# A two-layer hybrid trunk on one core: chunk scan by transition matrices, attention kept by token, substitution in PSUM, another step order, FFN sums copied from PSUM

## The chip, the cores and the metric

The kernel runs on one core of a Trainium2 chip. The metric is the device time of one execution in microseconds (us): the median of three runs of the kernel before was 2342.84 us (2339.17 to 2346.02). A profile was taken of one more execution.

## The reference, cut to what matters

Two layers work on a residual h of 512 tokens by 1024. In each, a feed-forward half-step (FFN a), a mixer, a second feed-forward half-step (FFN b) and a gated embedding (PLE) follow each other; the first three end in a layer norm. The mixer has three groups of heads on one projection: gated DeltaNet (8 heads of 64), stick-breaking attention (4 heads) and latent attention (4 heads). The change touches two of them:

```python
# DeltaNet, chunks of 64 tokens; lhs is unit lower triangular
u = triangular_solve(lhs, vc * beta)
w = triangular_solve(lhs, kb * exp(gc))
def step(state, xs):
    v_new = u_n - w_n @ state
    o_n = qd_n @ state + qk_n @ v_new
    state = state * gl_n + kd_n.T @ v_new
    return state, o_n
# latent attention, 4 blocks of 128 queries
s = (qn @ kn.T + qr @ kr.T) * scale, masked causally
o = softmax(s) @ v
```

## The kernel before, in words

All work is in `trunk`. TensorE (PE) multiplies; the precise products of weights are three fp32r matmuls (a high part, a low part and a cross part, L398 to L400 and L404 to L406), and the small products inside the heads are plain fp32, where one 64x64 matmul is two records in the trace. A framework puts the instructions into an order on each engine and sets the semaphores. Within the mixer the order that it starts from is the string `order` in `OPT`, one per layer, whose words are steps (`inv1` is `eliminate`, `uw2` is `u_w(2)`, `la13` is `latent(1, 3)`, `sc0` is `scan(0)`); the table `eng` says which engine copies or scales. PSUM is four pools of two banks: `psI` (`ibank()`, for the projections), `psA` (`bank()`), `psB` (`banks()`) and `psC` (`banks(True)`).

The steps that the change and the prediction touch, by their lines:

- **Inverse of lhs.** `inverse` (L911) turns the 16-row blocks onto partitions. `eliminate` (L926) does 15 steps of forward substitution on DVE, each a product (L936) and a sum (L937), on tiles `pr`, `X` and `inv_t` in SBUF. `turned` turns them back (L943, L944), and `inverse32` and `inverse64` double the block size with tiny matmuls (L955, L961). Beside it PE does the projection of the latents (`in_latent`), the values (`in_values`) and `keys`, whose transposes (L999) need the queries scaled by `decayed_queries` (`dq`, L893 on DVE).
- **u and w.** `u_w(t)` (L1000) makes u (L1007) and, with 64x64 products (L1016), w already transposed into `KQ`; a POOL multiplication (L643) scales by token in between.
- **Scan.** `scan(t)` goes through two chunks of 64 tokens. Per chunk: 16 matmuls with the old state (L1083), two DVE subtractions giving `vn`, 8 matmuls for the new state (L1096), a DVE sum, 8 matmuls on `vn` for the output (L1103), two ACT copies.
- **Latent attention.** `latent(h2, qt)` does two heads for 128 queries: scores (L801, L802), a maximum, its product with -scale (L805), exp on ACT with the sum, a division of the whole row of weights (L809), transposes (L811), a copy, and the product with the values (L818), whose result stands by channel.
- **Gates and out.** `gate_out` multiplies the normed scan output with the gate on POOL (L1133) and transposes it (L1166); `split_heads` makes high and low parts for the out-projection (L1139, L1140).
- **FFN front.** `build_xT(t)` transposes h (L258), and `split_from_psum` gives its high part by an ACT cast (L250) and its low part by DVE (L251). The FFN then sums the two parts again into `xf`, four pieces of 128x1024, two on POOL and two on DVE (L455), for the Strassen-like sums t1 to t4.

## Time and profile before

| what | value |
|---|---|
| median of three runs | 2342.84 us (2339.17 to 2346.02) |
| the profiled execution | 2345.6 us, its span 2343.9 us |
| mean granted TensorE clock | 0.976 of full speed |
| PE busy | 2265.5 us, 97% |
| DVE, ACT, POOL busy | 1379.9, 1043.0, 895.9 us (59, 44, 38%) |
| chain that ended last | PE 89%, DVE 7%, issue 2% |
| mixer of layer 0, of layer 1 | about 381 to 758 us, 1560 to 1920 us of the span |

PE is the engine to look at, but its 97% is a mean: in the FFNs it does not stop, and its idle time and its lower clock stand in the mixers and at the fronts of FFNs. A busy share of PE says nothing about the speed, so the granted clock belongs to each window. Where a line of a helper (L79, L250) stands in a row, the tile names tell which step called it.

### The profile page before, as it was taken

What the parts mean: (1) busy time and instruction counts of PE and PEld (TensorE: products, weight loads), DVE (VectorE), ACT (ScalarE), POOL (GpSimd) and SP (SyncE); (2) the same over time, 40 slices, a digit from 0 to 9 for tenths busy, and PEclk for the clock granted to TensorE, in tenths of its full rate; (3) what the DMA queues carried; (4) which work ended last, traced back from release to release, by engine and by line L of the source; (5) the groups of instructions that cost most, each with busy time, mean ns of one, the idle gap of its engine ahead of it and who ended that gap; (6) DMA issues with size and microseconds to landing.
All of it is one profiled execution on the core that took longest, in us unless ns stands there. A gap on an engine that the chain in (4) does not pass through costs nothing.

```text
span 2343.9 us, 40415 instructions
## 1 busy us (share of the span) xinstructions
PE 2265.5 (97%) x16834; PEld 1999.3 (85%) x16834; DVE 1379.9 (59%) x2027; ACT 1043.0 (44%) x1743; POOL 895.9 (38%) x491
## 2 busy tenths in 40 slices
PE   7999999998988999999999999999989889999999
PEld 7999888766877899988789998887678679999887
DVE  8877316657465877632667773166573758776333
ACT  4555423653442455532335554237534434556222
POOL 5222552433344522245442225524333554223442
PEclk9999999999989999999999999999989889999999
DMA  5332342212013133233413323422120121333331
GB/s 162 100 109 90 117 126 57 67 37 69 20 38 99 46 117 101 83 122 118 126 33 108 102 95 107 127 64 58 37 69 20 46 90 56 115 100 104 113 99 63
DMA packets 186792, 199.88 MB, mean 85 GB/s; under 512 B 10128, under 2 KB 151536, under 8 KB 186608
## 3 DMA queue, kind: packets, MB, share of 16 engines
q1 hardware_dynamic: 186608, 197.29, 27.7%
q8 instruction: 132, 2.16, 0.4%
q14 instruction: 52, 0.43, 0.1%
HBM read 195.17 MB, written 2.10 MB: 84 GB/s over the span
## 4 chain that ended last, share of the span: by engine, by line
PE 89%; DVE 7%; issue 2%; DMA 1%; POOL 1%; ACT 1%; SPq 0%; POOLq 0%; DVEq 0%; ACTq 0%
PE pi L398 6%; PE pi L400 6%; PE pi L399 6%; PE pc L406 4%; PE pc L405 4%; PE pc L404 4%; PE pa L406 3%; PE pa L405 3%; PE pa L404 3%; PE pb L405 3%; PE pb L406 3%; PE pb L404 3%; PE pc L398 2%; PE pc L399 2%; PE pc L400 2%; PE pi L406 2%
## 5 line engine op out<-in xcount | busy, mean ns | idle before, releaser
L79 POOL TENSOR_TENSOR wlo<-wraw,whi 128x1024 fp32r<-128x1024 f32 (+4 forms) x169 | 355.7, 2115 | 404.0 <-ACT whi L77 397.0
L77 ACT CAST whi<-wraw 128x1024 fp32r<-128x1024 f32 (+2 forms) x162 | 167.0, 1034 | 347.1 <-PE pa L400 176.7
L99 POOL TENSOR_TENSOR wlo<-wq,whi 128x1024 fp32r<-128x1024 f32 x48 | 126.2, 2629 | 288.2 <-ACT whi L98 275.8
L98 ACT CAST whi<-wq 128x1024 fp32r<-128x1024 f32 x116 | 121.7, 1049 | 132.2 <-issue 34.5
L99 POOL TENSOR_TENSOR wlo<-wraw,whi 128x1024 fp32r<-128x1024 f32 x32 | 86.1, 2691 | 226.3 <-ACT whi L98 178.1
L404 PE MATMUL pb<-x,whi 128*128 128x256 f32 x448 | 128.9, 290 | 2.1 <-ACT x L250 2.1
L405 PE MATMUL pb<-x,whi 128*128 128x256 f32 x448 | 130.0, 291 | 0.0
L406 PE MATMUL pb<-x,wlo 128*128 128x256 f32 x448 | 128.7, 288 | 0.0
L98 ACT CAST whi<-wraw 128x1024 fp32r<-128x1024 f32 x84 | 88.1, 1049 | 90.5 <-issue 25.5
L99 DVE TENSOR_TENSOR wlo<-wq,whi 128x1024 fp32r<-128x1024 f32 x68 | 87.1, 1281 | 68.0 <-ACT whi L98 68.0
L405 PE MATMUL pc<-x,whi 128*128 128x256 f32 x448 | 126.8, 284 | 0.0
L404 PE MATMUL pc<-x,whi 128*128 128x256 f32 x448 | 126.8, 284 | 0.0
L406 PE MATMUL pc<-x,wlo 128*128 128x256 f32 x448 | 126.5, 283 | 0.0
L98 ACT CAST whi<-s 128x1024 fp32r<-128x1024 f32 x80 | 83.8, 1048 | 62.5 <-PE pc L405 33.6
L99 DVE TENSOR_TENSOR wlo<-s,whi 128x1024 fp32r<-128x1024 f32 x80 | 110.8, 1385 | 1.3 <-ACT whi L98 1.2
L295 DVE SCALAR_TENSOR_TENSOR h<-h,pi 128x512 f32<-128x512 f32 x12 | 8.2, 684 | 167.3 <-PE pi L400 167.3
L398 PE MATMUL pi<-x,whi 128*128 128x512 f32 x256 | 103.8, 405 | 0.0
L400 PE MATMUL pi<-x,wlo 128*128 128x512 f32 x256 | 103.5, 404 | 0.0
L399 PE MATMUL pi<-x,whi 128*128 128x512 f32 x256 | 103.3, 403 | 0.0
L99 DVE TENSOR_TENSOR wlo<-wraw,whi 128x1024 fp32r<-128x1024 f32 x52 | 66.7, 1282 | 61.0 <-ACT whi L98 61.0
L406 PE MATMUL pi<-x,wlo 128*128 128x256 f32 x320 | 90.8, 284 | 3.9 <-POOL wlo L99 3.9
L406 PE MATMUL pa<-t,wlo 128*128 128x256 f32 x320 | 90.8, 284 | 1.7 <-DVE wlo L99 1.7
(549 smaller groups left out, 7839.4 us busy)
## 6 DMA issues: line engine op xcount, KB each, us to landing
wq<-in_ffa_w_in_dram SPq DMA_DIRECT2D x46, 512.0 KB, 3.8
wq<-in_ffb_w_in_dram SPq DMA_DIRECT2D x46, 512.0 KB, 3.6
wraw<-in_ffa_w_out_dram SPq DMA_DIRECT2D x44, 512.0 KB, 3.8
wraw<-in_ffb_w_out_dram SPq DMA_DIRECT2D x44, 512.0 KB, 3.6
wraw<-in_mix_w_in_dram SPq DMA_DIRECT2D x40, 512.0 KB, 3.9
wraw<-in_ffa_w_in_dram SPq DMA_DIRECT2D x34, 512.0 KB, 3.6
wraw<-in_ffb_w_in_dram SPq DMA_DIRECT2D x34, 512.0 KB, 3.6
wraw<-in_mix_w_o_dram SPq DMA_DIRECT2D x16, 512.0 KB, 3.8
```

What stands on the lines that cost most here:

```text
L77: self.nc.scalar.copy(hi[:, :width], raw[:, :width])
L79: (eng or self.nc.gpsimd).tensor_tensor(out=lo[:, c], in0=raw[:, c], in1=hi[:, c].bitcast(F32), op=ALU.subtract)
L98: nc.scalar.copy(hi, q[name])
L99: eng(name).tensor_tensor(out=lo, in0=q[name], in1=hi.bitcast(F32), op=ALU.subtract)
L295: V.scalar_tensor_tensor(out=hs, in0=hs, scalar=scale, in1=ps, op0=ALU.mult, op1=ALU.add)
L398: T.matmul(ps, ah, bh, start=first, stop=False)
L399: T.matmul(ps, ah, bl, start=False, stop=False)
L400: T.matmul(ps, al, bh, start=False, stop=last)
L404: T.matmul(dst, ah, bhl[:, 0], start=first, stop=False, skip_group_check=True)
L405: T.matmul(dst, ah, bhl[:, 1], start=False, stop=False, skip_group_check=True)
L406: T.matmul(dst, al, bhl[:, 0], start=False, stop=last, skip_group_check=True)
```

## The change

Five things, in both layers.

1. **Scan.** New steps `mv0` to `mv3` (`moves(t)`) turn each chunk into a linear map of the state: 32 matmuls of 64x64 give w-products with the keys and with the masked qk, subtracted from `KQ` by four DVE operations; 16 give the chunk's own contribution to the state (copied by ACT to `SB`), 16 the chunk's own output. `dm` fills decay times identity into `KQ` on POOL. What is left in `scan(t)` per chunk is 8 matmuls and one DVE sum for the state and 8 matmuls for the output, with two DVE sums per t. In `u_w` the second product keeps its rows and is copied once by ACT.
2. **Latent attention.** Scale and sign go into Q, the maximum becomes a minimum, the product L805 and the division L809 go; the last product has the weights stationary and 64 columns of values moving, and an ACT copy scales its result by token into `lo`; new steps `lo0` to `lo3` transpose it. `mxb` goes. The two head pairs use different PSUM pools.
3. **Substitution.** X is a PSUM bank, which ACT copies to SBUF before it is turned back; the products lie in `IA`.
4. **Order.** The two versions of the string from `pr1` on, the same in both layers:

```
before: v1 inv0 v0 dq inv1 inv2 lat_in keys in2 lh0 lh3 in3 lh2 v3 v2 qs uw0 uw1 lh1 uw2 la02 uw3 la11 la10 sc0 la13 gz0 sc1
        on1 sc2 sc3 on0 la00 mxa gz1 on2 go0 on3 go3 la03 la12 go1 la01 go2 mxb
after:  inv0 inv1 inv2 v1 v0 lat_in in2 v3 v2 keys dm lh0 in3 lh3 dq lh2 qs lh1 uw0 mv0 uw1 mv1 uw2 mv2 uw3 mv3 gz0 gz1 la00
        la10 lo0 la01 la11 lo1 mxa sc0 sc1 sc2 sc3 la02 la12 lo2 on0 go0 on1 go1 on2 go2 on3 go3 la03 la13 lo3
```

5. **Residual.** `build_xT` copies the transposed h from PSUM to `xf` by one more ACT copy of 128x512 per half, in the four places where an FFN follows; the sums L455 go, and the second half goes through a `psI` bank.

The diff, cut to these parts:

```diff
-    def new_xT():
+    def new_xT(ffn=False):
+
+        xT["full"] = [unit("xf"), unit("xf")] if ffn else None
         xT["x"] = xp.tile([P, 2, KD, S], F32R, tag="x", name=nm("x"))
         xT["hi"], xT["lo"] = xT["x"][:, 0], xT["x"][:, 1]
 
@@ -252,12 +257,17 @@
 
     def build_xT(t):
         for half in range(2):
-            ps = bank()
+            ps = ibank() if half and xT["full"] else bank()
             for k in range(4):
                 c = (half * 4 + k) * P
                 T.transpose(ps[:, k * P:(k + 1) * P], h[t][:, c:c + P], ident)
             sl = (slice(None), slice(half * 4, half * 4 + 4), slice(t * P, (t + 1) * P))
             split_from_psum(xT["hi"][sl], xT["lo"][sl], ps.rearrange("p (k c) -> p k c", k=4))
+            if xT["full"]:
+                A.copy(quarter_x(half, t // 2)[:, :, (t % 2) * P:(t % 2 + 1) * P], ps.rearrange("p (k c) -> p k c", k=4))
+
+    def quarter_x(i, j):
+        return xT["full"][j].rearrange("p a b -> p (a b)")[:, i * 1024:(i + 1) * 1024].rearrange("p (k c) -> p k c", k=4)
...
-        full = [unit("xf"), unit("xf")]
...
+        B = {(i, j): quarter_x(i - 1, j - 1) for i in (1, 2) for j in (1, 2)}
...
-            CP["qv"](qv[:, :, 0:64], pqv[:, :, 0:64])
+            A.activation(qv[:, :, 0:64], pqv[:, :, 0:64], AF.Copy, scale=-SC)
...
-            sc = float(96 ** -0.5)
             N = (qt + 1) * P
+            if qt not in lo:
+                lo[qt] = slab("lo", 256)
             for hp in range(2):
-                s = one(True)
+                s = one(h2 == 0)
                 hs = slice((2 * h2 + hp) * P, (2 * h2 + hp + 1) * P)
                 T.matmul(s[:, :N], QT[0:96, qt, hs], KT[0:96, 0:qt + 1, hs], start=True, stop=False)
                 T.matmul(s[:, qt * P:N], id_r, caus, start=False, stop=True)
-                mx, su = small("mx", 1, F32, 4), small("su", 1, F32, 4)
-                V.tensor_reduce(out=mx, in_=s[:, :N], op=ALU.max, axis=AX.X)
-                V.tensor_scalar(mx, mx, -sc, None, op0=ALU.mult)
-                p_, pT = MW[:, hp, :N], MW[:, 2 + hp, :N]
-                act(p_, s[:, :N], AF.Exp, scale=sc, bias=mx, accum_out=su)
+                mn, su = small("mx", 1, F32, 4), small("su", 1, F32, 4)
+                V.tensor_reduce(out=mn, in_=s[:, :N], op=ALU.min, axis=AX.X)
+                p_, pT = (MW[:, hp, :N], MW[:, 2 + hp, :N]) if h2 == 0 else (SVM[:, hp, :N], SQK[:, 2 + hp, :N])
+                act(p_, s[:, :N], AF.Exp, scale=-1.0, bias=mn, accum_out=su)
                 V.reciprocal(su, su)
-                EN["pscale"].tensor_scalar(p_, p_, su, None, op0=ALU.mult)
                 for kt in range(qt + 1):
                     T.transpose(s[:, kt * P:(kt + 1) * P], p_[:, kt * P:(kt + 1) * P], ident)
-                if hp:
-                    CP["pT1"](pT, s[:, :N])
-                else:
-                    CP["pT0"](pT, s[:, :N])
-                R = slice(hp * 64, hp * 64 + 64)
+                CP[f"pT{hp}"](pT, s[:, :N])
                 for kt in range(qt + 1):
-                    T.matmul(s[R, 0:P], vm[:, h2, kt, hp, :], pT[:, kt * P:(kt + 1) * P], start=kt == 0, stop=kt == qt)
-                CP["mo"](SQK[R, 2 + h2, qt * P:(qt + 1) * P], s[R, 0:P])
+                    T.matmul(s[:, 0:64], pT[:, kt * P:(kt + 1) * P], vm[:, h2, kt, hp, :], start=kt == 0, stop=kt == qt)
+                c = (2 * h2 + hp) * 64
+                A.activation(lo[qt][:, c:c + 64], s[:, 0:64], AF.Copy, scale=su)
+        def latent_out(t):
+            pp = bank()
+            for i in range(2):
+                T.transpose(pp[:, i * P:(i + 1) * P], lo[t][:, i * P:(i + 1) * P], ident)
+            ts_ = slice(t * P, (t + 1) * P)
+            split_from_psum(MXh[:, 2:4, ts_], MXl[:, 2:4, ts_], pp[:, 0:256].rearrange("p (k s) -> p k s", k=2))
...
-            X = lnp.tile([P, 1056], F32, tag="lnb", name=nm("X"))
-            G.memset(X, 0.0)
-            G.memset(X[:, 0:1024:33], 1.0)
-            G.memset(QZ, 0.0)
+            X = bank()
+            V.memset(X, 0.0)
+            for u in range(2):
+                V.memset(X[:, u * 256:(u + 1) * 256:17], 1.0)
...
-                tm = slab("inv_t", 512)
-                tv = tm[:, 0:2 * m * n].rearrange("p (u i c) -> p u i c", u=2, c=n)
+                tv = IA[:, 2 + j % 2, 0:2 * m * n].rearrange("p (u i c) -> p u i c", u=2, c=n)
                 row = blocks16(pr, j, j + 1, j + 1, 16)[:, :, 0, :].unsqueeze(3).broadcast_to([P, 2, m, n])
-                col = blocks16(X, j, j + 1, 0, n).broadcast_to([P, 2, m, n])
-                dst = blocks16(X, j + 1, 16, 0, n)
+                Xv = X.rearrange("p (u i c) -> p u i c", u=2, c=16)
+                col = Xv[:, :, j:j + 1, 0:n].broadcast_to([P, 2, m, n])
+                dst = Xv[:, :, j + 1:, 0:n]
                 V.tensor_tensor(out=tv, in0=row, in1=col, op=ALU.mult)
                 V.tensor_tensor(out=dst, in0=dst, in1=tv, op=ALU.add)
 
         def turned():
-            X = inv_s["X"]
+            X = lnp.tile([P, 1024], F32, tag="lnb", name=nm("X"))
+            G.memset(X, 0.0)
+            for u in range(2):
+                src = inv_s["X"][:, u * 256:(u + 1) * 256].rearrange("p (i c) -> p i c", c=16)
+                A.copy(X[:, u * 512:(u + 1) * 512].rearrange("p (i c) -> p i c", c=32)[:, :, 16 * u:16 * u + 16], src)
...
-            pw = banks()
-            for h2 in range(4):
+            pw = bank()
+            for hh in range(8):
                 for cp in range(2):
                     R = slice(cp * 64, cp * 64 + 64)
-                    for hp in range(2):
-                        c = (2 * h2 + hp) * 64
-                        T.matmul(pw[cp][hp * 64:hp * 64 + 64, h2 * 64:(h2 + 1) * 64], K[R, t, c:c + 64], EA[R, t, c:c + 64], start=True, stop=True)
+                    T.matmul(pw[R, hh * 64:(hh + 1) * 64], EA[R, t, hh * 64:(hh + 1) * 64], K[R, t, hh * 64:(hh + 1) * 64], start=True, stop=True)
+            CP["w"](EA[:, t, :], pw)
+            by_token(EN["by_K"], K[:, t, :], K[:, t, :], kd, t)
+
+
+
+        def decay_matrix():
             for i in range(2):
+                G.tensor_tensor(out=KQ[i].rearrange("p (h w) (c d) -> p h w c d", w=2, d=64)[:, :, 0], in0=id2.unsqueeze(1).unsqueeze(1).broadcast_to([P, 2, 8, 64]),
+                                in1=egl.rearrange("p (c h) -> p h c", h=4)[:, 2 * i:2 * i + 2, :].unsqueeze(3).broadcast_to([P, 2, 8, 64]), op=ALU.mult)
+
+        SB = IA
+
+        def moves(t):
+            pa = banks()
+            for hh in range(8):
+                h2, hp = hh // 2, hh % 2
                 for cp in range(2):
-                    CP["w"](KQ[i].rearrange("p (h w) s -> p h w s", h=2)[:, :, 0, t * P + cp * 64:t * P + cp * 64 + 64],
-                           pw[cp][:, i * 128:(i + 1) * 128].rearrange("p (h c) -> p h c", h=2))
-            by_token(EN["by_K"], K[:, t, :], K[:, t, :], kd, t)
+                    R = slice(cp * 64, cp * 64 + 64)
+                    Rh, c = slice(hp * 64, hp * 64 + 64), slice(hh * 64, (hh + 1) * 64)
+                    for w_, rhs in ((0, K), (1, EU)):
+                        T.matmul(pa[cp][Rh, w_ * 256 + h2 * 64:w_ * 256 + (h2 + 1) * 64], EA[R, t, c], rhs[R, t, c], start=True, stop=True)
+            for cp in range(2):
+                c0 = t * P + cp * 64
+                for i in range(2):
+                    kv = KQ[i].rearrange("p (h w) s -> p h w s", h=2)[:, :, :, c0:c0 + 64]
+                    V.tensor_tensor(out=kv, in0=kv, in1=pa[cp].rearrange("p (w h c) -> p h w c", w=2, h=4)[:, 2 * i:2 * i + 2], op=ALU.subtract)
+            for cp in range(2):
+                R = slice(cp * 64, cp * 64 + 64)
+                pb = bank()
+                for hh in range(8):
+                    h2, hp = hh // 2, hh % 2
+                    T.matmul(pb[hp * 64:hp * 64 + 64, h2 * 64:(h2 + 1) * 64], K[R, t, hh * 64:(hh + 1) * 64], Vt[R, t, hh * 64:(hh + 1) * 64], start=True, stop=True)
+                CP["o"](SB[:, t, cp * 256:(cp + 1) * 256], pb[:, 0:256])
+            pr_ = bank()
+            for hh in range(8):
+                for cp in range(2):
+                    R = slice(cp * 64, cp * 64 + 64)
+                    T.matmul(pr_[R, hh * 64:(hh + 1) * 64], EU[R, t, hh * 64:(hh + 1) * 64], Vt[R, t, hh * 64:(hh + 1) * 64], start=True, stop=True)
+            CP["o"](Vt[:, t, :], pr_)
...
         def scan(t):
...
+            po = banks()
             for cp in range(2):
                 c = 2 * t + cp
+                if not c:
+                    continue
                 R = slice(cp * 64, cp * 64 + 64)
                 c0 = t * P + cp * 64
...
+                old, new = (SB[:, x // 2, (x % 2) * 256:(x % 2 + 1) * 256] for x in (c - 1, c))
                 if c < 7:
                     ps = bank()
...
+                    for h2 in range(4):
+                        for hp in range(2):
+                            Rh = slice(hp * 64, hp * 64 + 64)
+                            T.matmul(ps[Rh, h2 * 64:(h2 + 1) * 64], kq(h2, 0)[Rh, c0:c0 + 64], old[Rh, h2 * 64:(h2 + 1) * 64], start=True, stop=True)
+                    V.tensor_tensor(out=new, in0=new, in1=ps[:, 0:256], op=ALU.add)
+                for h2 in range(4):
+                    for hp in range(2):
+                        Rh = slice(hp * 64, hp * 64 + 64)
+                        T.matmul(po[hp][R, h2 * 64:(h2 + 1) * 64], kq(h2, 1)[Rh, c0:c0 + 64], old[Rh, h2 * 64:(h2 + 1) * 64], start=True, stop=True)
+            R = slice(0 if t else 64, P)
+            for hp in range(2):
+                o = Vt[R, t, :].rearrange(HP, h2=4, hp=2)[:, hp]
+                V.tensor_tensor(out=o, in0=o, in1=heads(po[hp][R, 0:256], 4), op=ALU.add)
...
-        new_xT()
+        new_xT(True)
```

On PE, in layer 0 (pb, pa and pi are PSUM banks, K, EA, EU and V the tiles of keys, w, qk and values), this is the kernel before around the last product of `u_w`, with `KT,QT` rows of the latents ahead of it:

```order
3457 L400 MATMUL pi_6358<-whi_5765,x_3492 128x256
3458 L801 MATMUL pc_6025<-KT_3683,QT_3689 128x384
3459 L802 MATMUL pc_6025<-caus,id_r 128x128
3460 L801 MATMUL pc_6043<-KT_3683,QT_3689 128x384
3461 L802 MATMUL pc_6043<-caus,id_r 128x128
3462 L1016 MATMUL pb_6080<-EA_3678,K_3682 64x64 x2
3463 L1016 MATMUL pb_6081<-EA_3678,K_3682 64x64 x2
3464 L1016 MATMUL pb_6080<-EA_3678,K_3682 64x64 x2
3465 L1016 MATMUL pb_6081<-EA_3678,K_3682 64x64 x2
```

and this is the changed kernel from the end of `moves(2)` to the beginning of `moves(3)`:

```order
3637 L1050 MATMUL pb_6163<-EU_3697,EA_3684 64x64
3638 L1061 MATMUL pa_6200<-V_3696,K_3688 64x64 x8
3639 L1061 MATMUL pa_6210<-V_3696,K_3688 64x64 x8
3640 L1067 MATMUL pa_6220<-V_3696,EU_3697 64x64 x16
3641 L1022 MATMUL pa_6238<-V_3696,EA_3684 64x64 x16
3642 L1029 MATMUL pa_6257<-K_3688,EA_3684 64x64 x16
3643 L1050 MATMUL pb_6276<-K_3688,EA_3684 64x64
3644 L1050 MATMUL pb_6276<-EU_3697,EA_3684 64x64
3645 L1050 MATMUL pb_6277<-K_3688,EA_3684 64x64
3646 L1050 MATMUL pb_6277<-EU_3697,EA_3684 64x64
```

Before, latent products and, right behind the rows, weight products (`pi`) stand about the block. Now u_w(3) (L1022, L1029) stands between two blocks of moves, with no other matmul from row 3606 to 3676. An x2 of L1016 goes over two column halves of PE, and the bank changes the row half; in L1050 two matmuls follow each other in the same quarter (K, then EU).

On DVE, the kernel before inside `eliminate` (X is in SBUF, L893 is `dq`):

```order
466 L936 TENSOR_TENSOR inv_t_4997<-pr_4877,X_4878 128x78
467 L937 TENSOR_TENSOR X_4878<-X_4878,inv_t_4997 128x2x3x13
468 L936 TENSOR_TENSOR inv_t_5000<-pr_4877,X_4878 128x56
469 L893 TENSOR_TENSOR KQ_198_3684<-KQ_198_3684,pa_4953 128x512
470 L937 TENSOR_TENSOR X_4878<-X_4878,inv_t_5000 128x2x2x14
471 L936 TENSOR_TENSOR inv_t_5003<-pr_4877,X_4878 128x30
472 L893 TENSOR_TENSOR KQ_198_3684<-KQ_198_3684,pa_4957 128x512
473 L937 TENSOR_TENSOR X_4878<-X_4878,inv_t_5003 128x2x15
```

and the changed kernel at the end of `eliminate` (`pa` is the PSUM bank of X):

```order
465 L945 TENSOR_TENSOR IA_3702<-pr_4832,pa_4833 128x78
466 L946 TENSOR_TENSOR pa_4833<-pa_4833,IA_3702 128x2x3x13
467 L945 TENSOR_TENSOR IA_3702<-pr_4832,pa_4833 128x56
468 L946 TENSOR_TENSOR pa_4833<-pa_4833,IA_3702 128x2x2x14
469 L945 TENSOR_TENSOR IA_3702<-pr_4832,pa_4833 128x30
470 L946 TENSOR_TENSOR pa_4833<-pa_4833,IA_3702 128x2x15
471 L956 STREAM_TRANSPOSE IA_3702<-X_4872 128x32x32
472 L957 STREAM_TRANSPOSE DN_4876<-X_4872 128x32x32
```

`dq` has left the substitution, and two sums of values (L871) stand in it instead, further up.

On PE, the scan of the kernel before has blocks in which one row half (one bank) has several matmuls in a row, as at 684.72 us of the rows below, and one block in which the halves take turns:

```order
3706 L811 MATMUL pc_6665<-ident,MW_3692 128x128
3707 L811 MATMUL pc_6679<-ident,MW_3692 128x128
3708 L1083 MATMUL pb_6572<-state_3716,KQ_201_3687 64x64
3709 L1083 MATMUL pb_6573<-state_3716,KQ_201_3687 64x64
3710 L1083 MATMUL pb_6572<-state_3716,KQ_201_3687 64x64
3711 L1083 MATMUL pb_6573<-state_3716,KQ_201_3687 64x64
3712 L1083 MATMUL pb_6572<-state_3716,KQ_198_3684 64x64
3713 L1083 MATMUL pb_6573<-state_3716,KQ_198_3684 64x64
```

In the changed kernel the state's products stand so, between latent products:

```order
3705 L816 MATMUL pb_6698<-ident,SVM_3694 128x128 x2
3706 L1127 MATMUL pa_6737<-IA_3702,KQ_201_3693 64x64 x4
3707 L1127 MATMUL pa_6737<-IA_3702,KQ_198_3690 64x64 x4
3708 L410 MATMUL pi_7140<-whi_6360,MXl_3682 128x512
3709 L408 MATMUL pi_7140<-whi_6360,MXh_3692 128x512
3710 L409 MATMUL pi_7140<-wlo_6361,MXh_3692 128x512
3711 L816 MATMUL pb_6712<-ident,SVM_3694 128x128 x2
```

## Rows read from the trace of the kernel before

**Rows 1.** The page: busy time, share of the span and instructions of PE.

```profile
PE 2265.5 (97%) x16834; PEld 1999.3 (85%) x16834; DVE 1379.9 (59%) x2027; ACT 1043.0 (44%) x1743; POOL 895.9 (38%) x491
```

**Rows 2.** Windows: length; busy (instructions) of PE, PEld, DVE, ACT, POOL; clock, DMA share, GB/s.

```profile
400.00:800.00 400.00, 373.02 (x3327) 295.41 (x3326) 238.56 (x494) 182.19 (x379) 163.73 (x120) 0.93 0.18 52
1570.00:1970.00 400.00, 373.21 (x3386) 299.12 (x3385) 243.20 (x497) 183.76 (x384) 168.20 (x121) 0.94 0.18 53
...
540.00:600.00 60.00, 50.78 (x877) 39.75 (x875) 39.96 (x71) 20.67 (x40) 19.12 (x10) 0.86 0.23 68
600.00:680.00 80.00, 79.58 (x1137) 67.01 (x1138) 35.37 (x118) 36.63 (x107) 28.02 (x28) 1.00 0.09 28
680.00:760.00 80.00, 68.43 (x378) 53.51 (x372) 49.60 (x111) 30.65 (x59) 43.10 (x31) 0.87 0.28 81
```

**Rows 3.** Waits of PE, 530 to 770 us: us in total, times, longest.

```profile
PE pa L258 <- DVE h L312: 4.7, 1, 4.7
PE pc L811 <- DVE MW L809: 4.7, 3, 2.4
PE pa L1166 <- POOL GZ L1133: 4.6, 1, 4.6
PE pa L961 <- issue: 3.5, 2, 1.8
PE pa L999 <- DVE KQ L893: 3.4, 1, 3.4
```

**Rows 4.** Timeline of PE: start, duration, line, tiles, shape, count of records.

```profile
613.61 1.26 PE L1007 MATMUL pa<-V,EA 64*64 64x64 f32 x32
617.14 1.08 PE L791 MATMUL pc<-ident,MW 128*96 128x128 f32 x8
630.45 0.69 PE L1016 MATMUL pb<-EA,K 64*64 64x64 f32 x32
679.45 1.15 PE L1083 MATMUL pb<-state,KQ 64*64 64x64 f32 x32
684.72 1.90 PE L1083 MATMUL pb<-state,KQ 64*64 64x64 f32 x32
```

**Rows 5.** Lines, 533 to 572 us: shape and count; busy us, mean ns; idle before.

```profile
L400 PE MATMUL pi<-whi,x 128*128 128x416 f32 x25 | 9.0, 359 | 0.0
...
L936 DVE TENSOR_TENSOR inv_t<-pr,X 128x30 f32<-128x30 f32 (+7 forms) x15 | 8.0, 532 | 0.4
L937 DVE TENSOR_TENSOR X<-X,inv_t 128x30 f32<-128x30 f32 (+7 forms) x15 | 5.9, 391 | 0.4
L944 DVE STREAM_TRANSPOSE DN<-X 128x1024 f32<-128x1024 f32 x1 | 2.1, 2103 | 0.0
```

**Rows 6.** Timeline of DVE and POOL in the same stretch and behind it.

```profile
548.73 7.03 POOL L79 TENSOR_TENSOR wlo<-wraw,whi 128x1024 fp32r<-128x1024 f32 x3 [18.33 <-ACT whi L77]
548.79 2.42 DVE L936 TENSOR_TENSOR inv_t<-pr,X 128x78 f32<-128x78 f32 x1
572.99 2.32 DVE L830 SCALAR_TENSOR_TENSOR y<-pi,cw,y 128x511 f32<-128x511 f32 x3 [1.49 <-ACT y L827]
573.12 2.36 POOL L79 TENSOR_TENSOR wlo<-wraw,whi 128x1024 fp32r<-128x1024 f32 x1
```

**Rows 7.** Lines of the whole span: form and count; busy us, mean ns; idle before.

```profile
L809 DVE TENSOR_SCALAR MW<-MW,su 128x384 f32<-128x384 f32 (+3 forms) x32 | 23.0, 719 | 0.7
...
L250 ACT CAST x<-pa 128x512 fp32r<-128x512 f32 x64 | 36.7, 583 | 60.3 <-PE pa L258 54.8 <-PE pc L400 4.9
```

**Rows 8.** Timeline of POOL and DVE at an FFN's front and at the start.

```profile
768.28 2.89 POOL L455 TENSOR_TENSOR xf<-x 128x1024 f32<-128x1024 f32 x1 [1.47 <-DVE ln_nb L306]
772.44 2.85 DVE L312 TENSOR_TENSOR h<-h,lnb 128x512 f32<-128x512 f32 x1 [1.53 <-POOL h L311]
...
13.07 4.73 POOL L455 TENSOR_TENSOR xf<-x 128x1024 f32<-128x1024 f32 x2
15.51 2.37 DVE L600 TENSOR_TENSOR rp_a<-rp_f,rp_fr 128x64 f32<-128x64 f32 x1
```

More of the change, by code (lines that the diff above doesn't have):

```diff
@@ L230, in trunk @@
     V.tensor_scalar(tri_l, tri_u, -1.0, 1.0, op0=ALU.mult, op1=ALU.add)
+    id2 = cst.tile([P, 64], F32, name="id2")
+    V.tensor_tensor(out=id2, in0=ident[:, 0:64], in1=ident[:, 64:128], op=ALU.add)
     cpm = cst.tile([P, 2], F32, name="cpm")
@@ L903, in mixer @@
         EAf = EA.rearrange("p t (h f) -> p (t h) f", h=8)
-        IV = [U[n].rearrange("p a b -> p (a b)")[:, i * 1024:(i + 1) * 1024] for n in ("IA", "IB") for i in range(2)]
-        LC, DT, QZ, TS = (x.rearrange("p (n c) -> p n c", c=32) for x in IV)
+        IA = U["IA"]
+        LC, DT = (IA[:, i * 2:i * 2 + 2, :].rearrange("p a (n c) -> p (a n) c", c=32) for i in range(2))
         inv_s = {}
@@ L1092, in scan @@
+                old, new = (SB[:, x // 2, (x % 2) * 256:(x % 2 + 1) * 256] for x in (c - 1, c))
                 if c < 7:
                     ps = bank()
-                    for hh in range(8):
-                        h2, hp = hh // 2, hh % 2
-                        T.matmul(ps[hp * 64:hp * 64 + 64, h2 * 64:(h2 + 1) * 64], K[R, t, hh * 64:(hh + 1) * 64], vs[:, hh * 64:(hh + 1) * 64], start=True, stop=True)
-                    if c:
-                        V.tensor_tensor(out=new, in0=new, in1=ps[:, 0:256], op=ALU.add)
-                    else:
-                        V.tensor_copy(new, ps[:, 0:256])
@@ L1143, in mixer @@
                  "lat_in": in_latent, "lw": latent_weights, "in2": inverse32, "in3": inverse64, "keys": keys, "gz0": lambda: in_gz(0), "gz1": lambda: in_gz(1),
-                 "mxa": lambda: split_heads(0), "mxb": lambda: split_heads(2), "inv0": inverse, "inv1": eliminate, "inv2": turned}
+                 "mxa": lambda: split_heads(0), "inv0": inverse, "dm": decay_matrix, "inv1": eliminate, "inv2": turned}
         for t in range(NT):
```

60 lines of the change are left out of this document (17 added, 43 removed), and 4 rows, old and new, of the table OPT.

## The prediction

> **What bounds the kernel now.** I read the page first, for the busy shares: PE is busy for 2265.5 of 2343.9 us, 97% [rows 1], so work added to PE is paid for where PE is full, and only stretches in which it is not full can give time back. The windows say where those are: the two mixers, with 373 of 400 us busy and a granted clock of 0.93 and 0.94 [rows 2]. So each mixer has 27 us of idle time, and beside it a clock that is lower. Within the mixer of layer 0 the stretches differ: the inverse (540 to 600 us) has 9.2 us idle at 0.86, u, w and most of the scan (600 to 680) is full at 1.00, and the end of the scan with the gates (680 to 760) has 11.6 us idle at 0.87 [rows 2]. Then the waits of PE: five of them hold 20.9 us, one on the layer norm, three spells on the division of the latents' weights, one on the gate, two with no releaser among the tiny matmuls of the inverse, and one on `dq` [rows 3]. The second mixer is taken as the first; its window agrees within 0.2 us [rows 2].
>
> **PE's small products.** The prices are the durations of blocks of 32 records divided by 32 [rows 4]: 59 ns where one quarter of PE gets several matmuls in a row (L1083, the block of 1.90 us), 36 ns where two row halves take turns (L1083, 1.15 us), 39 ns where two diagonal quarters take turns (L1007), 22 ns where all four do (L1016). A matmul is two records. Both mixers together lose: L1083 448 records at 56 (six blocks of seven at 59, one at 36), 25.1 us; L1096 224 at 39 (two quarters take turns, no row of its own), 8.7; L1103 256 at 59 (one quarter), 15.1; L1016 256 at 22, 5.6. That is 54.5 us. They get: the moves' products with w, 512 records; with V 256 and 256; the new second product of u_w 256; the scan's 192 for the state and 224 for the output. The first stream gives each quarter two matmuls before it goes on (the order, rows 3643 to 3646). No row shows that pattern: 22 ns is its lower bound, 59 its upper, and I take 36, since the next quarter differs from the one that is running: 18.4 us. The others take turns between two quarters: 256 at 39 is 10.0 three times, the state 7.5; the output, half in a row and half in turns, at 47, is 10.5. That is 66.4 us, and 16 transposes for the latent output at 1.08 / 8 = 0.135 [rows 4] add 2.2. Where PE is full this counts in whole: **+14 us**, between +7 and +26. The 80 products of weights and values keep their number and have half the columns moving, but twice the stationary width; weight loads fill 85% of the span already [rows 1], so I take nothing for it, and half of 0.135 for 160 records, -11, as the bound.
>
> **The inverse.** The 30 operations of the substitution take 13.9 us of DVE and a turn 2.1 [rows 5]. Some of them took 2.42 us while POOL was splitting weights, against a mean of 0.39 for L937; an operation with one input in PSUM kept 2.32 / 3 = 0.77 us beside such a split [rows 5, 6]. With X in PSUM each of the 30 has an input there, so the three long ones (2.42 and two like it, some 6 us) should go. Of the edit that is off the path: `inv0` to `inv2` start earlier, and 97 weight products stand on PE between `products` and `inverse32`. With 359 ns busy each, overlapping their neighbours [rows 5], they cover between 17 and 35 us, against a chain of about 14 to 20 plus two ACT copies. So the substitution is hidden; without the cover, 3 us a mixer would come back. What ends is the wait on `dq`, 3.4 us, as `dq` now stands behind `keys` [rows 3]. The 3.5 us with no releaser belong to the tiny matmuls [rows 3] and stay. **-7 us** for two mixers, between 0 and -14 (those too).
>
> **No cover for the last moves.** The weight products of the gate are used up before `moves(2)` ends; u_w(3) and the moves beside it wait for ACT's copy of u, POOL's scaling by token, the copy of w, and the two banks of `psA`. The trace of before shows no such bare stretch. The nearest row is a spell of L811, 4.7 / 3 = 1.6 us from DVE to PE [rows 3]: about two such per mixer, 3.5 us, **+7 us**. The lower bound is nothing (latent products get in between), the upper four handovers, +13.
>
> **Latents.** The division costs DVE 23.0 us over 32 operations [rows 7], and PE waited 4.7 us for it in three spells [rows 3]. It goes; the scaling moves into an ACT copy behind the product, where only the next transposition waits. Two latent blocks now run in different pools, so one is computed while the other waits. I take 4 of the 4.7 us, **-8 us** for two; bounds 0 (another wait ends as late) and -18 (the 4.6 us on the gate go as well [rows 3]).
>
> **Clock.** In the two windows with idle time PE loses 50.78 x 0.14 + 68.43 x 0.13 = 16 us per mixer to the clock [rows 2], and they hold 20.8 us of idle time. Of that 3.4 + 4 - 3.5 = 3.9 us go, a fifth; so I give back a fifth of the loss, 3 us, **-6 us**; bounds 0 and -16.
>
> **FFN fronts.** The sums L455 go from POOL and DVE. After a mixer one of 2.89 us stood on POOL ahead of a norm's multiplication, and the following DVE operation took 2.85 us [rows 8]: 2 us for each of two mixers. At the start two sums took 4.73 us on POOL while a DVE operation of 64 elements took 2.37 [rows 8] ahead of the casts' low parts: 4 us. The layer norm's 4.7 us [rows 3] stay. In their place ACT gets 32 copies at the price of a cast, 0.583 us [rows 7], 4.7 us for each FFN; they stand behind the casts, and ACT is busy for under half of the span, so I take nothing, and as a bound two copies ahead of a cast at each front, +5. After the PLE I take 0. **-8 us**, between +5 and -14.
>
> `dm` and the smaller edits (rope tiles, constants) lie on POOL, ACT or DVE beside full PE and count as nothing; if `dm` came late, `moves(0)` would wait for the two operations.
>
> **Sum** against the profiled execution, 2345.6 us: 14 - 7 + 7 - 8 - 6 - 8 = **-8**, 2337.6. The median of the runs is 2.8 us below that execution, so the forecast is **2335 us**.
>
> **Rivals.**
> *Slower: the scan becomes a bare chain.* Seven times per mixer the state's matmuls wait for DVE's sum and DVE for them. Before, gate and latent products lay between chunks, and the stretch to 680 was full [rows 2]. Now the gate's are spent; only three latent blocks and twelve out-projections lie there. At one handover of 1.6 us [rows 3] a chunk, 11 us per mixer are added, +22: **2357 us**. For it: DVE was at 49.6 of 80 us and POOL at 43.1 in the following window [rows 2]; against it: the order still has latent products between the chunks. It decides once PE idles for over 11 us between the first and the last of the scan's products.
> *No change: the wait moves.* PE stops waiting for the division and waits as much longer for the gate, as DVE's normalisation and POOL's product end when they ended: the -8 of the latents falls, **2343 us**. For it: the gate's wait of 4.6 us stands right beside them [rows 3]; against it: DVE is rid of 23 us [rows 7].
> *Faster: the moves' product runs in all four quarters.* At 22 ns in place of 36, 512 records give 7 us more: **2328 us**. For it: L1016 has that price over the same four quarters; against it: there the quarter changes with every matmul, and a row of several in one quarter costs 59 [rows 4].
> The Trainium skill, "TensorEngine Tiling (Array Packing)", section Key Properties, says that different tiles of the array can load weights and multiply in parallel. By that rule alone this third rival would be the forecast. The trace agrees where quarters change each time (22 and 36 ns) and gives no such gain within a quarter (59 ns), which is why I stay in between.
>
> **How the numbers follow.** Forecast 0.38, slower rival 0.23, no change 0.22, faster rival 0.17. About 0.3% (7 us) is what a measurement of this kernel can tell from no change, so faster means below 2335.8 and slower above 2349.9. The forecast stands on the first border: of its 0.38, 0.24 count as faster, 0.14 as the same, for its gains are bounded wider than its costs. With the third rival's 0.16 and the lower edge of the second, 0.05, faster is 0.45; the rest of the second with the forecast's upper part is 0.30; slower is the first rival and the upper tails, 0.25. The forecast's own range is 2325 to 2345. The range reaches to 2312 (the third rival with clock and gate at their bounds) and to 2362 (the first with the moves' product near 59): 0.8 of the chance.
>
> **What would show it.** Right: no PE wait on `dq` or on a division; the substitution's operations all under 0.7 us beside POOL's splits; blocks of the moves' product of 32 matmuls (64 records) near 2.3 us; a few waits of 1 to 2 us in u_w(3) and moves(3); no POOL operation but the norm's ahead of an FFN. PE busy up by about 14 us less what the clock gives back, and idle down by some 4 us per mixer. Wrong: those blocks at 3.8 us; `inverse32` waiting for the turned X; idle in the scan over 11 us; casts of x waiting behind ACT's copies.

## The result, and the profile after

The changed kernel takes 2315.08 us (median of four runs, 2309.38 to 2323.06); the kernel before took 2344.43 us in the four runs beside it. The ratio is 0.9882, with a 95% interval of 0.9856 to 0.9908: **28 us less**, between 22 and 34. The forecast was 2335, 8 us less than the median of the three runs on which it was made. The sign was right and the time lies in the range, but the gain is more than three times the sum.

The page of the changed kernel, engine busy times (they answer to [rows 1]), and the two mixers' windows ([rows 2]; columns as there):

```profile
PE 2254.1 (97%) x17362; PEld 2001.4 (86%) x17362; DVE 1310.1 (57%) x1988; ACT 1059.9 (46%) x1751; POOL 854.9 (37%) x467
```

```profile
400.00:800.00 400.00, 377.40 (x3658) 306.42 (x3657) 215.40 (x480) 189.28 (x379) 157.97 (x113) 0.93 0.18 54
1570.00:1970.00 400.00, 379.52 (x3811) 312.78 (x3810) 232.00 (x489) 197.09 (x394) 162.71 (x113) 0.96 0.20 60
...
600.00:680.00 80.00, 72.19 (x1070) 60.68 (x1069) 27.71 (x99) 41.80 (x109) 34.10 (x29) 0.91 0.10 29
```

PE's busy time fell by 11.4 us where I had it rise (by 14, less what the clock gives back), and its idle time (span less busy) from 78.4 to 61.0 us. POOL and DVE have 41 and 70 us less to do. The mixers are not where most of the gain lies: the stretch from 600 to 680, full before, now has 7.8 us idle.

To find the place I cut both executions at the first transposition of h in each stretch, read from PE's timeline. Lengths in us:

| stretch | before | changed | difference |
|---|---|---|---|
| start, FFN a of layer 0 | 359.7 | 356.5 | -3.2 |
| mixer 0 | 398.4 | 395.7 | -2.7 |
| FFN b and first half of PLE | 353.4 | 348.4 | -5.0 |
| end of PLE, FFN a of layer 1 | 416.3 | 410.4 | -5.9 |
| mixer 1 | 390.8 | 384.0 | -6.8 |
| FFN b of layer 1 | 353.8 | 348.6 | -5.2 |
| last PLE | 71.5 | 71.5 | 0 |

The four stretches that begin with an FFN's front give 19.3 us, the two mixers 9.5. PE's idle time in the four fell from 34.9 to 16.3 us. These 19.3 us are firm, the 9.5 are not, as the profiled executions of the experiments below show. The four stretches together take 1480 to 1483 us in the three kernels with the front of before, and 1460 to 1464 in all ten with the new one. The two mixers together take 789 to 799 us in three kernels that have them as before, and 780 and 793 in two that have them as changed. This spread is the clock's: length times what the granted clock lacks of full speed (an estimate of the time lost to it) is 39 to 51 us in the first three, 43 and 60 in the other two. Without it the mixers take 748 to 751 us before and 737 and 733 changed, so they gain too, but mixer 1 against mixer 0 says nothing.

The front after mixer 0 shows how, in windows from the first transposition's surroundings to the FFN's first products. Before:

```profile
756.00:770.00 14.00, 8.53 (x38) 6.95 (x37) 13.24 (x27) 5.90 (x9) 9.00 (x8) 0.71 0.28 83
770.00:790.00 20.00, 20.00 (x162) 20.00 (x161) 18.15 (x15) 4.40 (x7) 7.70 (x4) 0.95 0.00 1
```

After:

```profile
748.00:764.00 16.00, 16.00 (x99) 14.03 (x98) 13.70 (x28) 7.87 (x13) 6.70 (x6) 1.00 0.31 98
764.00:784.00 20.00, 20.00 (x170) 20.00 (x169) 15.08 (x15) 11.58 (x16) 8.29 (x5) 1.00 0.17 56
```

PE was idle for 5.5 of 14 us and its clock at 0.71; now it neither stops nor slows. The wait of 4.7 us on the layer norm [rows 3], which I had left standing, is gone. In the order of time, the changed kernel's PE goes on with the out-projection between the transpositions, whose second half goes to another pool (`pi`, a bank of `psI`):

```profile
752.22 0.60 PE L263 MATMUL pa<-ident,h 128*128 128x128 f32 x4
752.57 0.48 PE L408 MATMUL pc<-w,MXh 128*128 128x512 f32 x1
...
754.50 0.60 PE L263 MATMUL pi<-ident,h 128*128 128x128 f32 x4
754.85 0.48 PE L410 MATMUL pc<-w,MGl 128*128 128x512 f32 x1
```

In the mixers the waits that I named are gone (the keys on `dq`, the division, the gate's product), and others took their places. The largest of these, in total over the span, and the scan's own wait (L1127):

```profile
PE pb L1050 <- POOL K L647: 5.5, 3, 3.1
PE pa L976 <- issue: 5.0, 3, 2.3
...
PE pa L1029 <- POOL EA L647: 4.4, 3, 2.0
PE pb L816 <- ACT SVM L184: 4.2, 3, 1.9
PE pb L808 <- DVE V L1136: 3.8, 2, 2.3
...
PE pa L1127 <- DVE IA L1128: 1.7, 2, 0.8
```

### The profile page after: what moved, and what is told of

It is laid out like the page before. It is cut to its first block, busy times and chain, and to the rows that moved or that the text cites. A ratio compares the mean times of both kernels' runs of the same rounds, so it can differ in the third digit from the quotient of the medians.

```text
span 2315.1 us, 41403 instructions
## 1 busy us (share of the span) xinstructions
PE 2254.1 (97%) x17362; PEld 2001.4 (86%) x17362; DVE 1310.1 (57%) x1988; ACT 1059.9 (46%) x1751; POOL 854.9 (37%) x467
## 4 chain that ended last, share of the span: by engine, by line
PE 90%; DVE 4%; POOL 2%; issue 2%; ACT 1%; DMA 1%; SPq 0%; POOLq 0%; DVEq 0%; ACTq 0%
PE pi L408 6%; PE pi L409 6%; PE pi L410 6%; PE pc L414 4%; PE pc L416 4%; PE pc L415 4%; PE pa L416 3%; PE pa L415 3%; PE pa L414 3%; PE pb L416 3%; PE pb L415 3%; PE pb L414 3%; PE pb L408 3%; PE pb L410 3%; PE pc L410 3%; PE pc L408 3%
## 5 line engine op out<-in xcount | busy, mean ns | idle before, releaser
L100 POOL TENSOR_TENSOR wlo<-wq,whi 128x1024 fp32r<-128x1024 f32 x48 | 121.4, 2529 | 291.6 <-ACT whi L99 291.6
L416 PE MATMUL pa<-x,wlo 128*128 128x256 f32 x320 | 91.8, 287 | 2.8 <-DVE wlo L100 2.8
L414 PE MATMUL pa<-x,whi 128*128 128x256 f32 x320 | 91.5, 286 | 0.0
L415 PE MATMUL pa<-x,whi 128*128 128x256 f32 x320 | 91.5, 286 | 0.0
```

Of the source, the lines that this page charges most:

```text
L100: eng(name).tensor_tensor(out=lo, in0=q[name], in1=hi.bitcast(F32), op=ALU.subtract)
L414: T.matmul(dst, ah, bhl[:, 0], start=first, stop=False, skip_group_check=True)
L415: T.matmul(dst, ah, bhl[:, 1], start=False, stop=False, skip_group_check=True)
L416: T.matmul(dst, al, bhl[:, 0], start=False, stop=last, skip_group_check=True)
```

## The experiments

Each kernel ran on one chip beside runs of the kernel before, whose medians lay between 2343 and 2346 us. So the ratios are compared; the last column is the ratio's difference from 0.9882 (or from 1), times 2344. An interval is 4 to 7 us wide on each side, and that of the changed kernel's own ratio is 6, so a difference from the changed kernel is uncertain by 7 to 9 us (an estimate from the two intervals): +15, +24, -14 and -11 stand clear of that, +9 is at its edge, and the others are not told from nothing by the time alone. The executions that were profiled are not always near the median (sums back 2346.5 us, before with the bank 2346.2, division back 2336.9), so their waits show where PE waits rather than how much in a median run.

| run | median us | ratio, 95% interval | against |
|---|---|---|---|
| sums back | 2333.06 | 0.9946, 0.9922 to 0.9970 | changed: +15 |
| before with the copy | 2327.71 | 0.9918, 0.9888 to 0.9948 | before: -19 |
| before with the bank | 2339.59 | 0.9969, 0.9951 to 0.9986 | before: -7 |
| division back | 2327.03 | 0.9916, 0.9887 to 0.9946 | changed: +8 |
| quarters in a row | 2340.58 | 0.9986, 0.9970 to 1.0001 | changed: +24 |
| X in SBUF | 2318.84 | 0.9906, 0.9884 to 0.9928 | changed: +6 |
| old inverse order | 2313.01 | 0.9869, 0.9845 to 0.9893 | changed: -3 |
| both of these | 2327.32 | 0.9919, 0.9894 to 0.9943 | changed: +9 |
| scan back | 2320.60 | 0.9885, 0.9860 to 0.9909 | changed: +1 |
| tokens on DVE | 2298.15 | 0.9822, 0.9794 to 0.9849 | changed: -14 |
| before, tokens on DVE | 2339.53 | 0.9979, 0.9965 to 0.9994 | before: -5 |
| tokens on DVE, moves interleaved | 2306.07 | 0.9836, 0.9813 to 0.9859 | changed: -11 |

### FFN fronts: the sums back, the copy alone, the bank alone

The changed kernel with the sums:

```diff
-        B = {(i, j): quarter_x(i - 1, j - 1) for i in (1, 2) for j in (1, 2)}
+        full = [unit("xf"), unit("xf")]
+        ...
+            (G if j == 1 else V).tensor_tensor(out=b, in0=XH[:, ks, cs].bitcast(F32), in1=XL[:, ks, cs].bitcast(F32), op=ALU.add)
-    new_xT(True)
+    new_xT()
```

> The changed kernel with its fifth part undone: x's high and low parts are summed again on POOL and DVE, no ACT copy, both halves of the transposed h through psA. Between the two profiles the four stretches that begin with an FFN's front lost 3.2, 5.0, 5.9 and 5.2 us, 19 us in all. Theory A, this part alone did that: about 2334 us, +19 on the changed kernel, and PE waits for the layer norm again at the front after each mixer. Rival B, most of it comes from the new order at the mixer's end (the norms start earlier) and only my -8 us from the sums: about 2323 us, +8.

The kernel before with the fifth part of the change:

```diff
-            ps = bank()
+            ps = ibank() if half and xT["full"] else bank()
+            if xT["full"]:
+                A.copy(quarter_x(half, t // 2)[:, :, (t % 2) * P:(t % 2 + 1) * P], ps.rearrange("p (k c) -> p k c", k=4))
```

> The kernel before with the fifth part alone: x copied from PSUM by ACT, second half through a psI bank, no sums. Theory A: 2325 us, -19 on the kernel before, the waits of PE on the layer norm at the FFN after the mixer gone. Rival B: 2336 us, -8, and the waits of 4.7 us on the layer norm stay.

And the kernel before with the bank alone:

```diff
-            ps = bank()
+            ps = ibank() if half and xT["ffn"] else bank()
```

> The kernel before with only the psI bank for the second half of the transposed h where an FFN follows; sums of the parts stay on POOL and DVE, no ACT copy. If the bank is what counts (a transposition no longer waits for the split of the one two ahead): -12 to -19 us, 2325 to 2332. If the sums on POOL and DVE are what counts, within 4 us of the kernel before.

The fifth part alone gives -19 us to the kernel before and its removal costs the changed one 15: theory A. The first number excludes rival B's -8, the second by itself hardly does (7 to 23). The lengths between first transpositions put it at the fronts: with the copy, the four stretches that begin with one take 356.7, 348.2, 411.8 and 346.3 us against 359.7, 353.4, 416.3 and 353.8 before, 20.2 less; with the sums back in the changed kernel they take 361.2, 353.1, 413.2 and 352.3, 15.9 more than in the changed kernel. The bank alone is worth 7 (its four stretches are 9 shorter), less than the 12 that I had for "the bank is what counts" and more than nothing; the rest, 12 (11 by the lengths), belongs to the sums, or to both together. What fails is one sign of theory A: with the sums back, PE does not wait for the layer norm again. Its waits on x and h in the whole span are these, of the kernel before and of the changed kernel with the sums:

```profile
PE pa L258 <- DVE h L312: 9.4, 2, 4.7
...
PE pa L258 <- DVE x L251: 6.3, 6, 2.6
...
PE pa L258 <- DVE h L1220: 3.3, 1, 3.3
```

```profile
PE pa L263 <- DVE x L256: 5.9, 5, 2.6
...
PE pa L263 <- DVE h L1258: 3.2, 1, 3.2
```

So the new order takes the norm's wait away by itself. The fifth part by itself takes about half of it: with the copy alone, 1.4 us on h and 3.6 on the norm's `ln_w` are left of 9.4. With the bank alone 5.5 are left, and there the waits on x fall from 6.3 to 1.4 us:

```profile
PE pa L260 <- DVE ln_w L309: 3.6, 2, 1.8
...
PE pi L260 <- DVE h L319: 1.2, 2, 0.9
```

```profile
PE pa L259 <- DVE ln_w L303: 3.6, 2, 1.8
...
PE pa L259 <- DVE x L252: 1.4, 1, 1.4
```

The waits on x and on the PLE's h come back without the copy and its bank. The second is the front that I priced at nothing: before, a transposition after the PLE waited 3.3 us, and the others came late, behind one another's splits in two banks; with the bank they lie between the gate products.

### Latents: the division back

```diff
                 V.reciprocal(su, su)
+                EN["pscale"].tensor_scalar(p_, p_, su, None, op0=ALU.mult)
...
-                A.activation(lo[qt][:, c:c + 64], s[:, 0:64], AF.Copy, scale=su)
+                A.activation(lo[qt][:, c:c + 64], s[:, 0:64], AF.Copy)
```

> The changed kernel with the division of the latents' weights put back on DVE ahead of the transpositions, and the copy behind the product unscaled. By my step on the latents, +8 us (2323), with PE waiting for the division again. Rival: those waits are covered or were replaced by others in the new order, where the stretch is bound elsewhere: within 3 us of the changed kernel.

+8 us, the size of the step, but inside what can be told (9 us). The trace is clearer: PE's waits before these transpositions (L817, in the changed kernel L816) are 15.2 us against 4.9, and these two among them the changed kernel does not have:

```profile
PE pb L817 <- DVE SVM L815: 4.1, 1, 4.1
PE pc L817 <- DVE su L814: 3.8, 4, 1.7
```

### The moves' product: quarters in a row

```diff
-            for hh in range(8):
-                h2, hp = hh // 2, hh % 2
-                for cp in range(2):
+            for hp, cp in ((0, 0), (0, 1), (1, 0), (1, 1)):
+                for h2 in range(4):
+                    hh = 2 * h2 + hp
```

> The changed kernel with the loops of the moves' first product turned: each quarter of PE gets eight matmuls in a row (hp, cp outside; h2, w_ inside) instead of two. Same matmuls, same result. In the changed kernel a block of 64 records took 1.31 us (20 ns a record). Theory: the price is set by how long one quarter is fed alone; the block then takes 64 x 59 ns = 3.8 us and the kernel, with 8 such blocks on a PE that is nearly full there, 12 to 20 us more (2327 to 2335). Rival: such runs overlap anyway once two quarters are near each other; block under 2 us, kernel within 4 us of the changed one.

In the changed kernel a block of 64 records goes by so (first and last rows; from 638.04 to 639.35, 1.31 us):

```profile
638.04 0.36 PE L1050 MATMUL pb<-K,EA 64*64 64x64 f32 x8
638.21 0.32 PE L1050 MATMUL pb<-EU,EA 64*64 64x64 f32 x8
638.33 0.33 PE L1050 MATMUL pb<-K,EA 64*64 64x64 f32 x6
...
639.13 0.22 PE L1050 MATMUL pb<-EU,EA 64*64 64x64 f32 x1
639.13 0.92 PE L1061 MATMUL pa<-V,K 64*64 64x64 f32 x30
```

and with eight in a row:

```profile
664.05 0.33 PE L1050 MATMUL pb<-K,EA 64*64 64x64 f32 x2 [1.19 <-POOL K L647]
664.22 0.28 PE L1050 MATMUL pb<-EU,EA 64*64 64x64 f32 x2
664.34 0.28 PE L1050 MATMUL pb<-K,EA 64*64 64x64 f32 x2
...
667.94 0.31 PE L1050 MATMUL pb<-EU,EA 64*64 64x64 f32 x1
```

Two records per 0.117 us, 59 ns each, but where one quarter gives way to the next (four records in the same time); the block shown takes 4.2 us, its last third at the lower clock. At the full clock a whole block takes 3.40 us, 53 ns a record, against 1.31. All eight keep PE busy for 33.6 us against 13.4, so 20 of the 24 us that the kernel loses (12 to 20 expected) are theirs: the theory holds, and with it the question that the prediction left between 22 and 59 ns is closed. Two in a row do not cost; eight do.

### The inverse: X in SBUF, the old order, both

```diff
-            X = bank()
+            X = slab("inv_t", 512)
```

> The changed kernel with X of the substitution in SBUF instead of a PSUM bank, in the same compact form and copied by ACT as before. By my step the substitution is hidden behind weight products, and only three or so DVE operations per mixer become 2 us longer beside POOL: within 3 us of the changed kernel, but DVE operations of 2.3 to 2.4 us in the substitution come back. Rival: the cover is too short and PE waits for the turned X: +4 to +12 us.

```diff
-inv0 inv1 inv2 v1 v0 lat_in in2 v3 v2 keys dm lh0 in3 lh3 dq lh2 qs lh1
+v1 inv0 v0 dq inv1 inv2 lat_in keys in2 lh0 lh3 in3 lh2 v3 v2 dm qs lh1
```

> The changed kernel with the steps around the inverse in the order of the kernel before (values and dq ahead of the substitution, keys ahead of inverse32), the rest of the order as changed. By my step +7 us (2322), with the wait of the keys' transposition on dq back at about 3 us in each mixer. Rival, from the profiles, in which the inverse stretch lost 2.2 us in one mixer and 8.2 in the other: between +2 and +14, as the clock falls or not.

Neither shows a loss that can be told from nothing (+6 and -3). With the old order, and X in PSUM, DVE goes through the substitution beside a POOL split without a change:

```profile
542.31 0.26 DVE L945 TENSOR_TENSOR IA<-pr,pa 128x96 f32<-128x96 f32 x1
...
542.60 0.27 DVE L946 TENSOR_TENSOR pa<-pa,IA 128x96 f32<-128x96 f32 x1
...
543.17 0.25 DVE L946 TENSOR_TENSOR pa<-pa,IA 128x78 f32<-128x78 f32 x1
```

```profile
542.37 7.13 POOL L80 TENSOR_TENSOR wlo<-wraw,whi 128x1024 fp32r<-128x1024 f32 x3 [17.49 <-ACT whi L78]
```

The wait of the keys on `dq` does not come back, so my expectation of 7 us fails. With the new order and X in SBUF, the substitution is through before the first split, and its operations have a mean of 253 and 255 ns. For both together:

> The changed kernel with both undone at once: the steps around the inverse in the old order, and X in SBUF. Alone, the old order cost nothing (DVE operations on X in PSUM kept 0.24 to 0.27 us beside a POOL split) and X in SBUF 3 us at most (with no POOL split during the substitution). Theory: either protects the substitution from POOL, so only both together bring back DVE operations of 2.3 us and a wait of PE on dq or the turned X: +5 to +12 us on the changed kernel (2320 to 2327). Rival: the inverse is worth nothing in either form: within 3 us.

+9 us, at the edge of what can be told, and the long operations are back, three of 2.3 to 2.4 us in the first mixer (means 532 and 391 ns over all, as before):

```profile
544.94 2.38 DVE L945 TENSOR_TENSOR IA<-pr,inv_t 128x110 f32<-128x110 f32 x1
547.36 2.35 DVE L946 TENSOR_TENSOR inv_t<-inv_t,IA 128x110 f32<-128x110 f32 x1
549.74 2.34 DVE L945 TENSOR_TENSOR IA<-pr,inv_t 128x96 f32<-128x96 f32 x1
```

Either edit is enough alone. What waits then is not what I expected: neither `dq` (0.3 us in a mixer) nor `inverse32`, but the latents' heads, for DVE, 7.6 us in both mixers (3.5 with the old order alone, none in the changed kernel); in the first mixer:

```profile
PE pc L769 <- DVE KT L764: 2.3, 1, 2.3
...
PE pc L769 <- DVE KT L765: 1.5, 1, 1.5
```

### The scan back

`u_w` and `scan` are those of the kernel before, and the moves and `dm` go:

```diff
-uw0 mv0 uw1 mv1 uw2 mv2 uw3 mv3 gz0 gz1
+uw0 uw1 uw2 uw3 gz0 gz1
```

> The changed kernel with its first part undone: u_w and scan of the kernel before (16, 8 and 8 matmuls per chunk, vn, decay on POOL), no moves, the rest as changed. On PE the small products of the two kernels take the same (54.5 us before, 52 after, the clock taken out). Theory A: the transition matrices are worth the shorter chain in the scan: 2320 to 2335, with waits of PE in the scan on DVE's vn. Rival B: they cost as much in bare u_w and moves as they save in the scan: within 4 us of the changed kernel.

+1 us: rival B, though with 8 us of uncertainty theory A's lower end is not excluded. As far as this can tell, the transition matrices neither gain nor lose in the new order. Without them PE waits in the scan instead:

```profile
PE pb L1098 <- DVE o_a L289: 8.9, 2, 4.5
...
PE pb L1098 <- DVE state L1113: 2.5, 10, 0.3
```

With them it waits in u_w and the moves for POOL (5.5 and 4.4 us, above).

### The scalings by token on DVE

```diff
-"by_EA": "G", "by_K": "G"
+"by_EA": "V", "by_K": "V"
```

> The changed kernel with the scalings by token of u_w (two per block of 128 tokens) on DVE instead of POOL. In the changed kernel PE waited 4.4 and 5.5 us for these POOL operations of about 1.05 us; DVE is free for two thirds of that stretch. If that wait is what bounds u_w and the moves: -5 to -10 us, 2305 to 2310. Rival: DVE's turn comes as late, or the scheduler had hidden the rest: within 3 us of the changed kernel.

> The kernel before with the scalings by token of u_w on DVE instead of POOL, which took 17 us off the changed kernel. There u_w and the moves have no other matmul between them. Theory: the gain belongs to that bare stretch; in the kernel before PE is full from 600 to 680 us, so within 4 us of the kernel before. Rival: POOL as such is what is saved, and the kernel before gains over 8 us too.

On the changed kernel it gives 14 us more (5 to 10 expected), the best of all versions (2298.15 us, 1.8% less than before); on the kernel before 5, between the two theories there. POOL took 1.04 and 1.10 us for one of these, DVE 0.87 to 0.89, so it is not the duration but the turn: POOL splits weights in between. In the changed kernel the longest wait came so; the scaling of K could begin when u_w's second product (L1029) ended at 648.8 us, and stood behind two splits and an operation of the gate:

```profile
649.07 2.48 POOL L80 TENSOR_TENSOR wlo<-wraw,whi 128x512 fp32r<-128x512 f32 x2
651.52 1.47 POOL L663 TENSOR_SCALAR e<-GZ 128x512 f32<-128x512 f32 x1
652.97 2.48 POOL L80 TENSOR_TENSOR wlo<-wraw,whi 128x512 fp32r<-128x512 f32 x2
655.42 1.48 POOL L647 TENSOR_TENSOR K<-K,kd 128x512 f32<-128x512 f32 x1
```

```profile
656.96 0.52 PE L1050 MATMUL pb<-K,EA 64*64 64x64 f32 x8 [3.15 <-POOL K L647]
```

With the scalings on DVE the waits on the scaled K are gone from the list, and those on EA have 3.4 us, 6.5 less for both. From the first product of u_w to the last of the moves the mixers take 60.6 and 61.2 us instead of 67.1 and 68.4, 13.7 less, at a clock of 0.96 and 0.95 instead of 0.90 and 0.89.

The order of the moves, on top of it:

```diff
-uw0 mv0 uw1 mv1 uw2 mv2 uw3 mv3
+uw0 uw1 mv0 uw2 mv1 uw3 mv2 mv3
```

> The changed kernel with the scalings by token on DVE and u_w one step ahead of the moves (uw0 uw1 mv0 uw2 mv1 uw3 mv2 mv3), so that between the two products of u_w another step's moves can stand. If what is left of waits in this stretch (3.4 us before L1029, 2.1 before L1061) goes: 2290 to 2295, 3 to 8 us less than with the scalings alone. Rival: the two banks of psA bound it in either order: within 3 us of 2298.

The intervals of the two overlap (0.9813 to 0.9859 against 0.9794 to 0.9849), so it isn't shown to be slower, but the expected gain of 3 to 8 us did not come. PE's waits on EA fell from 3.4 to 0.8 us and those before L1061 left the list; the waits on ACT's exp ahead of the latents' transpositions did not go:

```profile
PE pb L816 <- ACT SVM L184: 6.1, 6, 1.8
...
PE pc L816 <- ACT MW L184: 2.5, 3, 1.1
```

## Why the prediction was right in sign and short in size

Two steps failed, the price of the moves' first product and the fronts of the FFNs. Together they are 18 to 22 us, and the 8 forecast and the 28 measured are 20 apart; the other steps came near their prices or their misses cancel, as far as the runs can tell.

**PE's small products: +14 forecast, about +3 by the rows after.** The step that failed is the price of the moves' first product: 36 ns a record, chosen between 22 and 59. It measured 20 (1.31 us / 64), so 512 records are 10.2 us and not 18.4, at the full clock; three of the eight blocks run at a clock of 0.50 to 0.59 and take 1.9 to 2.2 us. The other streams were near their prices: u_w's second product 36 ns (1.15 us / 32, for 39), the state's own part 31 (0.92 / 30, for 39).

```profile
633.39 1.15 PE L1029 MATMUL pa<-K,EA 64*64 64x64 f32 x32
```

With these three the sum is 57 against 54.5 us. The busy times of all these lines, added up, say the same: 68.0 us before, 70.8 after. The products of weights and values, which I took at nothing, went from 20.5 to 23.6 us. The third rival named this mechanism and was right on it; and the experiment with eight in a row shows what the other end costs.

**The inverse: -7 forecast, -9 by the run with both edits undone.** The size holds within the 8 us of that run, the reason half: I gave the gain to `dq`'s place. The runs show that the long DVE operations beside POOL's splits come back only when both edits are undone; PSUM for X or the earlier place each removes them, and with X in PSUM `dq` may stand where it stood. That the wait on `dq` before (6.7 us in two mixers) followed from them is not shown: with both undone they are back, and that wait is 0.3 us a mixer. In the changed kernel no split runs beside the substitution (it ends at 544.31 us, the first split begins at 545.30), so the sign that I had named, short operations beside the splits, was put to the test only by the run with the old order.

**No cover for the last moves: +7 forecast.** The stretch from 600 to 680 us went from 0.4 to 7.8 us idle in mixer 0, twice what I had per mixer, with a clock of 0.91 where it was 1.00; the releaser that I named for it, POOL's scaling, leads the mixers' waits. Moving it to DVE gives 14 us. As a whole the first part, +21 by this step and the first, costs nothing that can be told (+1 when undone). That comparison is within the new order, where the old scan waits 11.4 us; in the kernel before, where it waited 0.4, it had other products beside it.

**Latents: -8 forecast, -8 measured** (the division back), with 9 us of uncertainty; the waits, 10 us more without the edit, bear it out.

**Clock: -6 forecast.** It came back elsewhere: in mixer 0 the mean clock of the window is 0.93 as before, in mixer 1 it rose from 0.94 to 0.96, and at the front after mixer 0 from 0.71 to 1.00. Reckoned as above, the two mixers lost 39 us to the clock before and 43 after, the four stretches with the fronts 17 and 3.

**FFN fronts: -8 forecast, -15 to -19 measured**, outside the bounds of the step (+5 to -14). This is the second step that failed. I counted the sums and two delays that I saw, priced the front after the PLE at nothing and left the layer norm's wait. Missed was the bank: two PSUM banks were shared by transpositions, each held until DVE's split was done, and two more let PE go on. Alone it is worth 7 us. I had read the bank in the diff and gave it no price, as no row says "waits for a bank": such a wait stands in the list as PE waiting for DVE's x, and with the bank alone it fell from 6.3 to 1.4 us. That the ACT copies would delay the casts did not happen to a measurable degree: PE's waits on the cast of x were 2.1 us in three before and are 1.7 in one.

**The rivals.** The bare scan did not decide: between the first and the last of the scan's products PE idles for 0.8 us in either mixer, where 11 was the sign, and the waits on the state's DVE sum are 1.7 us in both, not 22. "The wait moves" is true of names only.

The single runs add up to 15 to 19 (fronts), 8 (division), 9 (inverse) and 1 (scan), 33 to 37 against 28 measured; with some 8 us of uncertainty on each, and edits that share waits, this agrees. What stays open are the 12 us at the fronts between the sums and their meeting with the bank: the copy without the bank was not tried.

**The range.** That the time lies in it is partly luck. The low end, 2312, was drawn for the third rival with clock and gate at their bounds, and the fronts, which brought the time there, went beyond theirs. Both ends are also nearer than their parts give: 2328 - 10 - 10 = 2308 and 2357 + 12 = 2369.

## What to carry to other kernels

Give a PSUM bank a price when an edit adds one: look for every wait of PE on the engine that empties the tile, and count it as a wait on the bank. When POOL and DVE share SBUF work in a stretch, ask of each short operation on POOL what long one stands before it in its queue, and of each DVE operation whether one of its operands could lie in PSUM. Undo an edit alone and together with its neighbour: here two edits each seemed worth nothing, within the noise, because either removed the same long operations.
